# A projection's high weight half against both halves of its input at once

## Chip, cores and metric

The kernel runs on one core of a Trainium2 chip. The metric is the device time of one execution in microseconds; the figure for a kernel is the median of its runs.

## What is computed

Two transformer blocks over 256 tokens of width 1024, in float32. The first block ends in a convolutional gated feed-forward; the second begins with a mixer of two attentions (fox and NSA) whose outputs are merged by sigmoid gates. The change touches the up projection of the one and the merge gates of the other:

```python
def conv_glu_ffn(xn, w_up, conv_w, conv_b, w_down):      # xn = rmsnorm(x), d_ff = 2816
    gu = xn @ w_up
    gate, up = jnp.split(gu, 2, axis=-1)
    gate = causal_dwconv(gate, conv_w) + conv_b.astype(gate.dtype)
    return (jax.nn.silu(gate) * up) @ w_down
...
def hybrid_mixer(h, w_in, ...):                          # h = rmsnorm_2(x)
    proj = h @ w_in
    ...
    g = jax.nn.sigmoid(merge_logit).reshape(B_, S_, N_BRANCH, D_MODEL)
    up = jnp.einsum('bsnc,ncd->bsnd', ys, w_branch)
    merged = jnp.sum(g * up, axis=2)
    return merged @ w_out
```

## The kernel before

Activations lie feature-major: 128 features on the partitions, 8 chunks of them for the width 1024, and the 256 tokens (T) along the free dimension. TensorE multiplies in a reduced format (fp32r), so each float32 operand is split into a high half (the value rounded to fp32r) and a low half (the rest), and each product is three matmuls that add up in one PSUM tile: high weight by high input, high weight by low input, low weight by high input (`mm3`, L346 to 351).

Weights stream in 128x1024 pieces, 4 buffers of each kind: a DMA on SP's queue brings a raw piece `w` (`wraw`), ScalarE copies it to its high half `wh`, and VectorE subtracts to get the low half `wl` (`whalf`, L328). Where the stretch is not marked `calm`, every third subtract goes to GpSimd.

One call of `fm_pair` (L375) makes two chunks of 128 output features for all 256 tokens: 2 chunks x 8 input chunks x 3 matmuls of 128x256, into one 128x512 PSUM tile. The input is the pair of halves of the normed activations, two tiles `xnh` and `xnl` of [128, 8, 256]. The gain is in the halves already; the reciprocal root mean square `r` of each token is multiplied in afterwards, by `fm_norm` (L406), with one VectorE multiply in PSUM (L411), so the projections can start before `r` is known.

There are 8 PSUM banks, 4 buffers called `acc` and 4 called `att`, each 128x512.

In `ffn` (L728) the 4 `acc` buffers hold the output of the down projection over the whole stage. The 22 ups work in `att` buffers: up k makes one chunk of gates and one of ups, so that two ups feed one down. After the multiply by `r`, VectorE does the width-3 convolution of the gate chunk into `fg` (one tensor_scalar, L741, and two multiply-adds, L743), ScalarE the Silu, VectorE the product with the other chunk into `fa` (L746), and after each second up the split of `fa` into `anh` and `anl`. Ups 0 and 1 are done by other helpers since they begin while the norm is still being made; ups 2 to 21 call `fm_norm`. `ffn_order` places a down after each even up from 2 on (down 0 after up 2's issue), the last three at the end. Only the ups up to 3 and from 19 on are `calm`.

In `block2` eight calls of `merge(j)` make the gates, each by `fm_norm` into an `acc` buffer and a ScalarE Tanh into `mg`. They are issued among the steps of the NSA attention: scores on TensorE, maxima on VectorE (L1734), exponentials on ScalarE, reciprocals and scalings on VectorE (L1738, L1743), transposes and the product with the values on TensorE. Between merges 0 and 2 also stands a small softmax over compressed blocks (`L`, L976 to 988), transposed on TensorE (L995) and copied to `PC`.

The order on each engine is set by the Tile scheduler, which places the instructions by its own timeline model; on each engine they then run in that order. A PSUM or SBUF tile's buffer is taken again when all readers of its last holder are done.

Of the kernel before, what the change touches and what calls it, by code (L numbers as in the profile page):

```python
# [21 lines left out]
T = 256  # L22
# [277 lines left out]
class Prog:  # L300
# [89 lines left out]
    def fm_quad(self, x, order, late):  # L390
# [7 lines left out]
                         k == order[0] and c == 0, k == order[-1], skip_group_check=True)  # L398
        return ps

    def first_pair(self, n, **k):

        ps, n.first = n.first or self.fm_pair(n.halves, **k), None
        return ps
# [84 lines left out]

    def pre_norm(self, x, gain):  # L490

        n = Normed(x, *[self.npool.tile([128, 8, T], F32R, tag="xn" + t, name="xn" + t) for t in "hl"])
        self.gain_halves(n, gain)
        return n

# [35 lines left out]
    def post_norm(self, gain):  # L531

        nc, x = self.nc, self.x
        if self.part:
            hs = [self.whalf() for _ in range(2)]
            first = [self.att((128, 512)) for _ in range(2)][::-1]
            self.fm_pair(self.old.halves, ps=first[0], hs=hs)
            self.fm_pair(self.part[1:], ps=first[1], hs=hs)
        n = Normed(x, *[self.npool.tile([128, 8, T], F32R, tag="xn" + t, name="xn" + t) for t in "hl"])
        r = self.rstd(self.pms, self.ptable)  # L540
        self.table = self.ptable
        bc = r[:, None, :].to_broadcast([128, 2, T])
        with self.tc.manual_schedule(engines={mybir.EngineType.DVE}):
            for p in range(5):
                if p < 4:
                    xp, hp = x[:, 2 * p:2 * p + 2], self.hg[:, 2 * p:2 * p + 2]
                    nc.vector.tensor_mul(hp, hp, bc)
                    nc.vector.tensor_add(xp, xp, hp)
                    for k in (2 * p, 2 * p + 1):
                        self.act(n.halves[0][:, k], x[:, k], AF.Identity, scale=gain[:, k:k + 1])  # L550
                for k in (2 * p - 2, 2 * p - 1) if p else ():
                    nc.vector.scalar_tensor_tensor(n.halves[1][:, k], x[:, k], gain[:, k:k + 1],
                                                   n.halves[0][:, k].bitcast(F32), op0=ALU.mult, op1=ALU.subtract)
            if self.part:
                f = [t.rearrange("p (a b) -> p a b", a=2) for t in first]
                t = self.npool.tile([128, 2, T], F32, tag="sq", name="t", bufs=3)
                nc.vector.tensor_mul(t, f[1], bc)
                nc.vector.tensor_add(f[0], f[0], t)
                n.first, self.part = first[0], None
        return n  # L560
# [31 lines left out]
    def build(self):  # L592
        tc, nc = self.tc, self.nc
        with ExitStack() as es:
            pool = lambda name, bufs=1, **k: es.enter_context(tc.tile_pool(name=name, bufs=bufs, **k))
            self.cpool = pool("consts")
            self.pacc = pool("pacc", 4, space=PSUM)
            self.patt = pool("patt", 4, space=PSUM)
            self.dpool = pool("dpool", space=DRAM)
            self.epsc = self.cpool.tile([128, 1], F32, name="epsc")  # L600
            nc.vector.memset(self.epsc, EPS)
            with ExitStack() as big:
                xpool = big.enter_context(tc.tile_pool(name="xpool", bufs=1))
                self.wpool = big.enter_context(tc.tile_pool(name="wpool", bufs=1))
                self.npool = big.enter_context(tc.tile_pool(name="npool", bufs=1))
                self.vec = xpool.tile([128, self.a["vec"].shape[1]], F32, name="vec")
                x = self.x = xpool.tile([128, 8, T], F32, name="x")
                self.table = nc.scalar.preload_act_table_set("natural_log_exp_and_others")
                self.ones = xpool.tile([128, T], F32, name="ones")
                nc.vector.memset(self.ones, 1.0)  # L610
                self.onesd = xpool.tile([128, 128], F32, name="onesd")
                nc.vector.memset(self.onesd, 1.0 / D)

                idle = self.att((128, T))
                for _ in range(8):
                    nc.tensor.matmul(idle, self.onesd, self.ones, start=True, stop=True)

                nc.sync.dma_start(self.vec, self.a["vec"])
                n = Normed(x, *[self.npool.tile([128, 8, T], F32R, tag="xn" + t, name="xn" + t) for t in "hl"])
                gain = self.v("norm_mix_pre")  # L620
                w = self.wpool.tile([128, 1024], F32, tag="w", name="w", bufs=4)
                hi, lo = [self.wpool.tile([128, 1024], F32R, tag=t, name=t, bufs=4) for t in ("wh", "wl")]
                for j in range(2):
                    nc.sync.dma_start(x[:, 4 * j:4 * j + 4], self.a["xT"][:, j * 1024:(j + 1) * 1024])
                    if j == 0:
                        nc.sync.dma_start(w, self.a["W"][0][:, :1024])
                for j in range(2):
                    part = slice(j * 512, j * 512 + 512)
                    nc.vector.tensor_copy(hi[:, part], w[:, part])
                    nc.vector.tensor_sub(lo[:, part], w[:, part], hi[:, part].bitcast(F32))  # L630
                    for k in range(4 * j, 4 * j + 4):
                        self.split(n.halves[0][:, k], n.halves[1][:, k], x[:, k], gain[:, k:k + 1])
                self.wi = 1
                self.ahead = [(hi, lo), self.whalf()]
                self.bd64 = xpool.tile([128, 128], F32, name="bd64")
                nc.gpsimd.memset(self.bd64, 0.0)
                for i in (0, 64):
                    nc.gpsimd.memset(self.bd64[i:i + 64, i:i + 64], 1.0 / 64)
                first = [self.fm_pair(n.halves) for _ in range(2)]
                self.norm_sums(n)  # L640
                self.calm = False
                self.sw = self.cload(xpool, "sw")
                self.c = self.cload(xpool, "cst")
                self.io = self.cload(self.cpool, "cst3")
                self.ident = self.cpool.tile([128, 128], F32, name="ident")
                nc.gpsimd.tensor_copy(self.ident, self.c("ident"))
                n = self.block1_mixer(n, first)
                n = self.cross(n)
                n = self.ffn(n)
                self.block2(n)  # L650
                self.hfp = pool("hfp", side="right")
                self.uvx = es
                self.peer_q()
            self.peer()
# [72 lines left out]

    def ffn(self, n):  # L728
        tc, nc, act = self.tc, self.nc, self.act
        with tc.tile_pool(name="ffn", bufs=1) as fp:  # L730
            hps = [self.acc() for _ in range(4)]
            an, early = {}, []

            def up(k):
                if k % 2 == 0:
                    an[k // 2] = fp.tile([128, 2, T], F32, tag="fa", name="fa", bufs=3)
                if k < 2 and not early:
                    early.extend([self.first_pair(n), self.fm_pair(n.halves, ps=self.att((128, 512)), outer=True)])
                ps = self.fm_norm(n, ready=early[k]) if k < 2 else self.fm_norm(n, ps=self.att((128, 512)))
                g = fp.tile([128, T], F32, tag="fg", name="fg", bufs=3)  # L740
                nc.vector.tensor_scalar(g, ps[:, :T], self.v("fconv2", k), self.v("ffn_conv_b", k), op0=ALU.mult, op1=ALU.add)  # L741
                for d in (1, 2):
                    nc.vector.scalar_tensor_tensor(g[:, d:], ps[:, :T - d], self.v(f"fconv{2 - d}", k), g[:, d:],  # L743
                                                   op0=ALU.mult, op1=ALU.add)
                act(g, g, AF.Silu)
                nc.vector.tensor_mul(an[k // 2][:, k % 2], g, ps[:, T:])  # L746
                if k % 2:
                    an[k // 2] = self.halves(fp, an[k // 2], "an", 3)
# [21 lines left out]
    def block2(self, n):  # L770
# [4 lines left out]
        with tc.tile_pool(name="b2", bufs=1) as bp:  # L775
# [8 lines left out]
            with tc.tile_pool(name="b2a", bufs=1) as ap:  # L784
# [166 lines left out]


                def merge(j):
                    ps = self.fm_norm(n)
                    act(fl(mg[:, 2 * j:2 * j + 2]), ps, AF.Tanh, scale=0.5)


                vb2 = vb.rearrange("p a d -> p (a d)")
# [420 lines left out]
    def block1_mixer(self, n, first):  # L1379
# [4 lines left out]
        with tc.tile_pool(name="mix", bufs=1) as mp:  # L1384
# [293 lines left out]
            for _ in range(2):  # L1678
                step(memory)

            hi, lo = [self.npool.tile([128, 8, T], F32R, tag="xn" + t, name="y" + t) for t in "hl"]
            for j in (3, 1, 2, 0):
                self.split(hi[:, 2 * j:2 * j + 2], lo[:, 2 * j:2 * j + 2], y[:, 2 * j:2 * j + 2])
            order = (6, 7, 2, 3, 4, 5, 0, 1)
# [124 lines left out]
```

## Time and profile before

| | |
|---|---|
| median of 3 runs | 1478.99 us |
| the runs | 1477.73, 1478.99, 1482.02 us |
| the profiled execution's own time | 1478.34 us |
| its span in the profile | 1476.6 us |
| mean granted clock of TensorE | 0.994 |
| TensorE busy | 1437.5 us, 97% of the span |
| VectorE busy | 1079.0 us, 73% |
| ScalarE busy | 782.2 us, 53% |
| GpSimd busy | 223.3 us, 15% |
| instructions | 26774 |

The busy time of an engine is the union of its instructions' spans. Matmuls are pipelined: the recorded length of one (0.28 us for 256 columns) is longer than the interval to the next, so the cost of a matmul in a stream is read from start to start. In the rows below PE is TensorE, DVE VectorE, ACT ScalarE, POOL GpSimd; L411 is line 411; `128x256` is partitions by elements; a bracket at the end gives the idle time before an instruction and what ended it.

### The profile page before, as it was taken

Reading aid. Unit: us, or ns where it says so; the run is one execution under the profiler, and the core shown is the slowest. Engines: PE = TensorE matmul, PEld = TensorE weight load, DVE = VectorE, ACT = ScalarE, POOL = GpSimd, SP = SyncE. Lnnn points to the kernel's source line nnn. Section 1 sums busy time; section 2 is a strip of 40 time slices with the busy share of each in tenths; the row PEclk is TensorE's granted clock in tenths of the full one; section 3 lists DMA queues with packets and bytes.
Section 4 is the critical chain, followed back from the end, with each engine's and each line's share of the span. In section 5 each row is a group of like instructions: output and inputs, shape, how many; then the busy total and the mean of one; then the engine's idle time right before and its main releaser. Section 6 shows DMA issues by size and latency. Waiting matters only on the chain.

```text
span 1476.6 us, 26774 instructions
## 1 busy us (share of the span) xinstructions
PE 1437.5 (97%) x10614; PEld 1336.2 (90%) x10614; DVE 1079.0 (73%) x1996; ACT 782.2 (53%) x1315; POOL 223.3 (15%) x139
## 2 busy tenths in 40 slices
PE   8899898999999999999899999999999999999997
PEld 7798888999999899999899999999998888888886
DVE  7768688766777656669988889778887555655555
ACT  7446466444556756556444545544445445454554
POOL 3731000232200431106341220000000000000000
PEclk9999999999999999999999999999999999999999
DMA  7443432555655433355355545545546555555553
GB/s 255 147 154 116 135 122 86 173 184 179 193 169 192 157 99 131 119 196 177 123 183 163 167 152 185 167 160 170 163 166 221 192 194 191 199 190 195 190 197 128
DMA packets 68245, 246.64 MB, mean 167 GB/s; under 512 B 7540, under 2 KB 8568, under 8 KB 67864
## 3 DMA queue, kind: packets, MB, share of 16 engines
q1 hardware_dynamic: 67544, 243.10, 49.6%
q8 instruction: 83, 1.36, 0.4%
q10 hardware_dynamic: 576, 1.84, 0.3%
q14 instruction: 42, 0.34, 0.1%
HBM read 242.80 MB, written 2.10 MB: 166 GB/s over the span
## 4 chain that ended last, share of the span: by engine, by line
PE 75%; DVE 9%; ACT 1%; issue 1%; POOL 0%; ACTq 0%; DVEq 0%
PE acc L349 20%; PE acc L350 20%; PE acc L351 20%; PE att L350 3%; PE att L351 3%; PE att L349 3%; PE att L1255 2%; DVE wl L328 1%; DVE uvl L1109 1%; PE att L1724 1%; PE acc L1762 1%; DVE ti L1033 1%; DVE tmp L1031 1%; PE att L1751 1%; ACT wh L370 0%
## 5 line engine op out<-in xcount | busy, mean ns | idle before, releaser
L1109 DVE TENSOR_TENSOR uvl<-uv,uvh 128x1024 fp32r<-128x1024 f32 x234 | 291.2, 1244 | 153.5 <-ACT uvh L370 153.3
L370 ACT ACTIVATE uvh<-uv 128x1024 fp32r<-128x1024 f32 x256 | 270.1, 1056 | 235.6 <-PE acc L350 131.1
L370 ACT ACTIVATE wh<-w 128x1024 fp32r<-128x1024 f32 x187 | 196.0, 1057 | 191.5 <-PE acc L350 89.0
L351 PE MATMUL acc<-hh,uvl 128*128 128x256 f32 x1024 | 289.8, 283 | 5.3 <-DVE uvl L1109 4.3
L349 PE MATMUL acc<-hh,uvh 128*128 128x256 f32 x1024 | 294.0, 287 | 0.0
L350 PE MATMUL acc<-hl,uvh 128*128 128x256 f32 x1024 | 289.9, 283 | 0.0
L328 DVE TENSOR_TENSOR wl<-w,wh 128x1024 fp32r<-128x1024 f32 x146 | 184.1, 1267 | 80.1 <-ACT wh L370 79.0
L351 PEld LDWEIGHTS acc<-hh,uvl 128*128 128x128 f32 x1024 | 196.0, 191 | 6.1 <-DVE uvl L1109 4.9
L350 PE MATMUL acc<-uvl,ch 128*128 128x512 f32 x512 | 199.2, 389 | 0.0
L351 PE MATMUL acc<-uvh,cl 128*128 128x512 f32 x512 | 199.2, 389 | 0.0
L350 PEld LDWEIGHTS acc<-hl,uvh 128*128 128x128 f32 x1024 | 196.1, 192 | 0.0
L349 PEld LDWEIGHTS acc<-hh,uvh 128*128 128x128 f32 x1024 | 196.0, 191 | 0.0
L349 PE MATMUL acc<-xnh,wh 128*128 128x256 f32 x544 | 157.3, 290 | 4.7 <-ACT wh L370 3.2
L351 PE MATMUL acc<-xnh,wl 128*128 128x256 f32 x544 | 155.0, 285 | 1.9 <-POOL wl L328 1.2
L350 PE MATMUL acc<-xnl,wh 128*128 128x256 f32 x544 | 155.1, 285 | 0.2
L328 POOL TENSOR_TENSOR wl<-w,wh 128x1024 fp32r<-128x1024 f32 x41 | 100.4, 2448 | 354.3 <-ACT wh L370 352.3
L349 PE MATMUL acc<-uvh,ch 128*128 128x512 f32 x512 | 138.5, 389 | 0.0
L350 PEld LDWEIGHTS acc<-uvl,ch 128*128 128x128 f32 x512 | 96.1, 188 | 19.9
L349 PEld LDWEIGHTS acc<-uvh,ch 128*128 128x128 f32 x512 | 96.1, 188 | 19.9
L351 PEld LDWEIGHTS acc<-uvh,cl 128*128 128x128 f32 x512 | 96.1, 188 | 20.0
L349 PEld LDWEIGHTS acc<-xnh,wh 128*128 128x128 f32 x544 | 104.3, 192 | 8.3 <-ACT wh L370 3.8
L351 PEld LDWEIGHTS acc<-xnh,wl 128*128 128x128 f32 x544 | 104.6, 192 | 3.5 <-POOL wl L328 1.4
(434 smaller groups left out, 2956.4 us busy)
## 6 DMA issues: line engine op xcount, KB each, us to landing
w<-in_W_dram SPq DMA_DIRECT2D x188, 512.0 KB, 4.3
uv<-in_U_dram SPq DMA_DIRECT2D x128, 512.0 KB, 3.6
uv<-in_V_dram SPq DMA_DIRECT2D x128, 512.0 KB, 3.5
mg<-in_cw_dram SPq DMA_DIRECT2D x4, 512.0 KB, 6.9
x<-in_xT_dram SPq DMA_DIRECT2D x2, 512.0 KB, 3.6
mem<-in_memT_dram SPq DMA_DIRECT2D x1, 1024.0 KB, 6.8
sk<-in_W_dram SPq DMA_DIRECT2D x1, 1024.0 KB, 7.5
xd<-xt SPq DMA_DIRECT2D x2, 512.0 KB, 3.1
```

What stands on the lines that cost most here:

```text
L328: (self.nc.gpsimd if pool else self.nc.vector).tensor_tensor(out=lo, in0=w, in1=hi.bitcast(F32), op=ALU.subtract)
L349: mm(ps, wsl(w[0]), xsl(x[0]), start=first, stop=False, **k)
L350: mm(ps, wsl(w[0]), xsl(x[1]), start=False, stop=False, **k)
L351: self.last_mm = mm(ps, wsl(w[1]), xsl(x[0]), start=False, stop=last, **k)
L370: return self.nc.scalar.activation(out, in_, f, **k)
L1031: nc.vector.match_replace(tmp[:, :n], vals[:, 0:8], src, -3.0e38)
L1033: nc.vector.max_index(idx[:, 0:8], vals[:, 0:8], src)
L1109: i = (nc.gpsimd if lo_pool else nc.vector).tensor_tensor(out=lo, in0=w, in1=hi.bitcast(F32), op=ALU.subtract)
L1255: mm(ps[:, j], m1[:, j], m2[:, s * NT + j], start=s == 0, stop=s == 1)
L1724: m = mm(S[i][:, part[blk]], q[rows[i], ch, blk * 128:(blk + 1) * 128], k[rows[i], br if nsa else ch, :128 * (blk + 1)], start=blk == 1, s ...
L1751: nc.tensor.transpose(pt[:, j * 128:(j + 1) * 128], P[:, i, j * 128:(j + 1) * 128], self.ident)
L1762: m = mm(po[rows[i], ch % 2, 128 * blk:], v[:, blk, vc:vc + 64], PT[i][:, 256 * blk:256 + 128 * blk], start=not nsa and blk == 0, stop=blk ...
```

## The change

A new helper `normed` allocates the two halves of the normed input in one tile, [128, 8, 2, 256], so that high and low half of a chunk lie side by side and can be read as 512 consecutive columns. Everything that used the two tiles now uses two strided views of the one.

A new helper `fm_side` takes the place of `fm_norm` in ups 2 to 21 and in the merges. For each of its two chunks it takes a PSUM buffer of its own. For each of the 8 input chunks it issues two matmuls: high weight by both halves, 128x512, whose first 256 columns are the product with the high half and whose last 256 that with the low half; and low weight by the high half, 128x256, added onto the first 256 columns. On the way out ScalarE copies the last 256 columns to SBUF, VectorE adds the first 256 from PSUM, and after both chunks VectorE multiplies by `r` in SBUF. In the ups the result lies in a new SBUF tile `fs` (3 buffers) that the convolution reads; in the merges in `mg` itself, on which Tanh then works in place.

```diff
+    def normed(self, name):
+        t = self.npool.tile([128, 8, 2, T], F32R, tag="xn", name=name)
+        return t[:, :, 0], t[:, :, 1]
+
+    def fm_side(self, n, get, out):
+        mm, (xh, xl) = self.nc.tensor.matmul, n.halves
+        both = [bass.AP(tensor=xh.tensor, offset=xh[:, k].offset, ap=[xh.ap[0], [1, 2 * T]]) for k in range(8)]
+        hs = [self.whalf() for _ in range(2)]
+        for c, (wh, wl) in enumerate(hs):
+            ps = get()
+            for k in range(8):
+                sl = slice(k * 128, k * 128 + 128)
+                mm(ps, wh[:, sl], both[k], start=k == 0, stop=False, skip_group_check=True)
+                self.last_mm = mm(ps[:, :T], wl[:, sl], xh[:, k], start=False, stop=k == 7, skip_group_check=True)
+            self.act(out[:, c], ps[:, T:], AF.Copy)
+            self.nc.vector.tensor_add(out[:, c], out[:, c], ps[:, :T])
+        self.norm_sums(n)
+        self.nc.vector.tensor_mul(out, out, n.r[:, None, :].to_broadcast([128, 2, T]))
...
-        n = Normed(x, *[self.npool.tile([128, 8, T], F32R, tag="xn" + t, name="xn" + t) for t in "hl"])
+        n = Normed(x, *self.normed("xn"))
...
     def ffn(self, n):
...
-                ps = self.fm_norm(n, ready=early[k]) if k < 2 else self.fm_norm(n, ps=self.att((128, 512)))
+                if k < 2:
+                    ps = self.fm_norm(n, ready=early[k])
+                else:
+                    ps = fp.tile([128, 2, T], F32, tag="fs", name="fs", bufs=3)
+                    self.fm_side(n, lambda: self.att((128, 512)), ps)
+                    ps = fl(ps)
...
                 def merge(j):
-                    ps = self.fm_norm(n)
-                    act(fl(mg[:, 2 * j:2 * j + 2]), ps, AF.Tanh, scale=0.5)
+                    o = mg[:, 2 * j:2 * j + 2]
+                    self.fm_side(n, self.acc, o)
+                    act(fl(o), fl(o), AF.Tanh, scale=0.5)
```

In the changed kernel `fm_side` is L406 to 421 and the lines behind it are 22 to 29 higher: the feed-forward's multiply-adds are L771, the product into `fa` L774, the attention's maxima L1763, the reciprocal L1767.

How the instructions stand now is shown at three places. The first is TensorE at the start of up 2, right behind the two matmuls that sum the squares for `r` (`sq`). Before:

```order
L351 MATMUL att<-xnh,wl 128x256
L477 MATMUL att<-sq,onesd 128x256 x2
L349 MATMUL att<-xnh,wh 128x256
L350 MATMUL att<-xnl,wh 128x256
L351 MATMUL att<-xnh,wl 128x256
L349 MATMUL att<-xnh,wh 128x256
```

and of the change:

```order
L351 MATMUL att<-xn,wl 128x256
L499 MATMUL att<-sq,onesd 128x256 x2
L416 MATMUL att<-xn,wh 128x512
L417 MATMUL att<-xn,wl 128x256
L416 MATMUL att<-xn,wh 128x512
```

Two matmuls stand for three, and the order of TensorE's work around them is otherwise the same but for the places where other work is let in between.

The second is VectorE at the start of the ups, from the end of the computation of `r`. Before:

```order
L452 SCALAR_TENSOR_TENSOR rstd<-nt,rstd 128x256
L411 TENSOR_TENSOR att<-att,rstd 128x512 x2
L741 TENSOR_SCALAR fg<-att,vec 128x256 x2
L328 TENSOR_TENSOR wl<-w,wh 128x1024
L743 SCALAR_TENSOR_TENSOR fg<-att,vec,fg 128x255 x2
L411 TENSOR_TENSOR att<-att,rstd 128x512
L743 SCALAR_TENSOR_TENSOR fg<-att,vec,fg 128x254 x2
```

and of the change:

```order
L474 SCALAR_TENSOR_TENSOR rstd<-nt,rstd 128x256
L433 TENSOR_TENSOR att<-att,rstd 128x512 x2
L769 TENSOR_SCALAR fg<-att,vec 128x256 x2
L328 TENSOR_TENSOR wl<-w,wh 128x1024
L771 SCALAR_TENSOR_TENSOR fg<-att,vec,fg 128x255
L419 TENSOR_TENSOR fs<-fs,att 128x256
L771 SCALAR_TENSOR_TENSOR fg<-att,vec,fg 128x255
L771 SCALAR_TENSOR_TENSOR fg<-att,vec,fg 128x254
L328 TENSOR_TENSOR wl<-w,wh 128x1024
L419 TENSOR_TENSOR fs<-fs,att 128x256
```

The two adds of up 2 (L419, into `fs`) stand among the convolution's operations of ups 0 and 1, the first of them behind a low half and one multiply-add.

The third is VectorE at merges 1 and 2, from the sum of the small softmax (`st`, `L`) to the reciprocal of an attention step (`attR`). Before:

```order
L983 TENSOR_REDUCE st<-L 128x16
L984 TENSOR_TENSOR L<-L,cst_5047 128x256
L985 RECIPROCAL st<-st 128x16
L986 TENSOR_TENSOR st<-st,gt 128x16
L411 TENSOR_TENSOR acc<-acc,rstd 128x512
L988 TENSOR_TENSOR L<-L,st 128x256
L328 TENSOR_TENSOR wl<-w,wh 128x1024
L1734 TENSOR_REDUCE attR<-att 128x1 x4
L1738 RECIPROCAL attR<-attR 128x4
```

and of the change:

```order
L1014 RECIPROCAL st<-st 128x16
L328 TENSOR_TENSOR wl<-w,wh 128x1024
L419 TENSOR_TENSOR mg<-mg,acc 128x256
L1015 TENSOR_TENSOR st<-st,gt 128x16
L1763 TENSOR_REDUCE attR<-att 128x1 x2
L421 TENSOR_TENSOR mg<-mg,rstd 128x512
L1017 TENSOR_TENSOR L<-L,st 128x256
L1763 TENSOR_REDUCE attR<-att 128x1 x2
L328 TENSOR_TENSOR wl<-w,wh 128x1024
L419 TENSOR_TENSOR mg<-mg,acc 128x256
L1767 RECIPROCAL attR<-attR 128x4
```

A low half (L328) and the add of a chunk of merge 2 (L419) now stand between the maxima and the reciprocal of the attention step.

The queues of SP and GpSimd hold the same instructions in the same order as before.

## Rows read from the trace of the kernel before

**Rows 1.** Page, section 1: busy us (share of the span) xinstructions.

```profile
PE 1437.5 (97%) x10614; PEld 1336.2 (90%) x10614; DVE 1079.0 (73%) x1996; ACT 782.2 (53%) x1315; POOL 223.3 (15%) x139
```

**Rows 2.** Windows, 272 to 437, 531 to 612: length; busy by engine; clock; DMA.

```profile
272.00:437.00 165.00, 164.89 (x1382) 164.77 (x1381) 114.68 (x162) 78.32 (x100) 34.10 (x14) 1.00 0.58 185
531.00:612.00 81.00, 81.00 (x702) 74.58 (x702) 50.22 (x120) 50.09 (x117) 16.16 (x11) 1.00 0.37 120
```

**Rows 3.** Waits of PE, 250 to 452: total us, times, longest.

```profile
PE att L477 <- DVE sq L464: 2.5, 1, 2.5
PE att L350 <- DVE xnl L552: 2.4, 2, 2.0
```

**Rows 4.** Timeline of PE, a projection of block 2: start us, us, instruction.

```profile
488.01 0.28 PE L349 MATMUL acc<-xnh,wh 128*128 128x256 f32 x1
...
492.57 0.28 PE L351 MATMUL acc<-xnh,wl 128*128 128x256 f32 x1
```

**Rows 5.** Timeline of PE, a 512-wide projection.

```profile
474.04 0.39 PE L351 MATMUL acc<-wh,xnl 128*128 128x512 f32 x1
...
477.67 0.39 PE L349 MATMUL acc<-wh,xnh 128*128 128x512 f32 x1
```

**Rows 6.** Timeline of PE, both widths side by side.

```profile
486.95 0.39 PE L351 MATMUL acc<-wh,xnl 128*128 128x512 f32 x1
487.18 0.28 PE L351 MATMUL acc<-xnh,wl 128*128 128x256 f32 x1
487.29 0.28 PE L349 MATMUL acc<-xnh,wh 128*128 128x256 f32 x1
```

**Rows 7.** Timeline of ACT, at merge 2.

```profile
557.90 1.06 ACT L370 ACTIVATE wh<-w 128x1024 fp32r<-128x1024 f32 x1 [1.07 <-issue]
558.86 0.37 ACT L370 ACTIVATE PC<-att 128x256 f32<-128x256 f32 x1
```

**Rows 8.** DVE groups by form, 272 to 437: busy us, mean ns; idle.

```profile
L411 DVE TENSOR_TENSOR att<-att,rstd 128x512 f32<-128x512 f32 x19 | 13.2, 697 | 7.8 <-PE att L351 7.7
...
L746 DVE TENSOR_TENSOR fa<-fg,att 128x256 f32<-128x256 f32 x20 | 8.4, 418 | 5.1 <-ACT fg L370 5.1
```

**Rows 9.** Timeline of DVE, the last ups.

```profile
409.10 0.70 DVE L411 TENSOR_TENSOR att<-att,rstd 128x512 f32<-128x512 f32 x1 [0.30 <-PE att L351]
...
413.01 1.22 DVE L328 TENSOR_TENSOR wl<-w,wh 128x1024 fp32r<-128x1024 f32 x1 [0.58 <-ACT wh L370]
...
414.86 0.70 DVE L411 TENSOR_TENSOR att<-att,rstd 128x512 f32<-128x512 f32 x1 [0.30 <-PE att L351]
```

**Rows 10.** Timeline of DVE, start of the ups.

```profile
263.88 1.21 DVE L328 TENSOR_TENSOR wl<-w,wh 128x1024 fp32r<-128x1024 f32 x1
265.01 0.86 DVE L743 SCALAR_TENSOR_TENSOR fg<-att,vec,fg 128x255 f32<-128x255 f32 x2
```

**Rows 11.** Timeline of PE, first matmul of up 2; down 0.

```profile
258.98 0.47 PE L349 MATMUL att<-xnh,wh 128*128 128x256 f32 x1
...
272.15 0.39 PE L350 MATMUL acc<-anl,wh 128*128 128x256 f32 x1
```

**Rows 12.** Timeline of DVE, at merge 1.

```profile
556.33 1.01 DVE L1743 TENSOR_SCALAR attP<-attP,attR 128x128 f32<-128x128 f32 x4
```

**Rows 13.** Timeline of PE, at merge 2.

```profile
559.17 0.50 PE L1751 MATMUL att<-ident,attP 128*128 128x128 f32 x3
```

**Rows 14.** Timeline of PE, a projection matmul behind transposes.

```profile
507.39 0.36 PE L349 MATMUL acc<-xnh,wh 128*128 128x256 f32 x1
507.59 0.28 PE L350 MATMUL acc<-xnl,wh 128*128 128x256 f32 x1
```

**Rows 15.** Timelines of DVE and POOL, 319 to 334.

```profile
320.23 0.68 DVE L341 TENSOR_TENSOR anl<-fa,anh 128x512 fp32r<-128x512 f32 x1
...
330.45 2.47 DVE L341 TENSOR_TENSOR anl<-fa,anh 128x512 fp32r<-128x512 f32 x1 [1.83 <-ACT anh L370]
...
329.98 2.40 POOL L328 TENSOR_TENSOR wl<-w,wh 128x1024 fp32r<-128x1024 f32 x1 [6.12 <-ACT wh L370]
```

More of the change, by code (lines that the diff above doesn't have):

```diff
@@ L538, in post_norm @@
             self.fm_pair(self.part[1:], ps=first[1], hs=hs)
-        n = Normed(x, *[self.npool.tile([128, 8, T], F32R, tag="xn" + t, name="xn" + t) for t in "hl"])
+        n = Normed(x, *self.normed("xn"))
         r = self.rstd(self.pms, self.ptable)
@@ L618, in build @@
                 nc.sync.dma_start(self.vec, self.a["vec"])
-                n = Normed(x, *[self.npool.tile([128, 8, T], F32R, tag="xn" + t, name="xn" + t) for t in "hl"])
+                n = Normed(x, *self.normed("xn"))
                 gain = self.v("norm_mix_pre")
@@ L729, in ffn @@
         tc, nc, act = self.tc, self.nc, self.act
+        fl = lambda t: t.rearrange("p a b -> p (a b)")
         with tc.tile_pool(name="ffn", bufs=1) as fp:
@@ L1679, in block1_mixer @@
                 step(memory)
-            hi, lo = [self.npool.tile([128, 8, T], F32R, tag="xn" + t, name="y" + t) for t in "hl"]
+            hi, lo = self.normed("y")
             for j in (3, 1, 2, 0):
```

## Prediction

> **What bounds the kernel now.** I began with the busy shares of the page: TensorE is busy for 1437.5 us of the 1476.6 us span and no other engine comes near [rows 1]. A share is an average, so the next view is that of windows, cut at the two stretches that the change touches [rows 2]. In the ups and downs of the feed-forward (272 to 437 us) TensorE is busy 164.89 of 165.00 us, in the stretch of the merge gates (531 to 612 us) 81.00 of 81.00, both at a granted clock of 1.00. The reader is to see that VectorE (114.68 of 165) and ScalarE (78.32) have room there, and that no transfer is waited for. The view of waits agrees: TensorE's two long waits between 250 and 452 us end before the third up [rows 3]. So here a nanosecond taken from TensorE's own stream is a nanosecond of the end, until something new makes TensorE wait.
>
> **What a k-step costs now and after.** Before, a step is three 128x256 matmuls. In an unbroken run of such matmuls, of another projection of the same input, the first starts at 488.01 and the 39th at 492.57 us: 4.56 us over 38 intervals, 0.120 us each [rows 4]; a step is 0.360 us. After, it is one 128x512 and one 128x256 matmul. The trace has unbroken 128x512 matmuls from a third projection: 17 of them from 474.04 to 477.67 us, 3.63 over 16 intervals, 0.2269 us [rows 5]. The two forms also stand side by side: after a 512-wide start the next, 256-wide one starts 0.23 us later, and the one behind that 0.11 us later [rows 6], so changing width has no price of its own. The new step is 0.2269 + 0.120 = 0.347 us, and saves 0.240 - 0.2269 = 0.0131 us. The columns streamed are the same (768 a step); what goes is one fixed share of a matmul, some 13 ns, and one weight load, which ran beside the matmuls anyway.
>
> There are 20 ups (k = 2 to 21) and 8 merges, each of 2 chunks by 8 steps: 448 steps, of which 320 in the ups and 128 in the merges. 448 x 0.0131 = **5.9 us saved**: 4.2 in the ups, 1.7 in the merges.
>
> The Trainium skill (TensorE: Matmul & The Clock Gate, section Back-to-back issue gap) speaks against this: its formula for the isolated gap is the columns over 2.4 GHz and a constant 2.5 ns, an estimate of 109 ns for 256 columns and 216 for 512. By it a step would save 2.5 ns and the change 1.1 us. The rows have 120 and 227, and the sum goes by the rows.
>
> **What is added.** Each of the 56 chunks gets a ScalarE copy of 128x256 out of PSUM and a VectorE add of the other 256 columns. A like copy took 0.37 us [rows 7], a like VectorE operation with one operand in SBUF and one in PSUM 418 ns; the wide multiply, which now works in SBUF, took 697 ns [rows 8]. So 0.37 us of ScalarE and about 0.42 us of VectorE a chunk (0.70 at most), 0.84 us of VectorE an up. Nothing is taken off for operations that now read SBUF in place of PSUM. Both engines have idle time: VectorE needs 114.68 of 165 us now, and 19 ups add 0.84 x 19 = 16. Priced at zero where TensorE does not wait, and what hides it is TensorE's own stream of matmuls. Its cover is thinnest in the last ups, where VectorE makes all low halves: one up there has a period of 5.76 us with 0.58 + 0.30 idle [rows 9], so it would be 5.76 - 0.88 + 0.84 = 5.72 us, against TensorE's 16 x 0.347 = 5.55. That is 0.17 short an up, for the last three ups; three chunks of slack (3 x 2.78 = 8.3 us) and the last downs take it. SP's and GpSimd's queues keep their order, so no transfer and no GpSimd subtract moves; the other users of the shared halves keep their operations, with a strided operand, priced at zero with the same cover.
>
> **Where TensorE will newly wait.** Every chunk now takes a PSUM buffer to itself, so four buffers hold two ups and not four.
>
> First, the start of the ups. Up 3's first chunk takes the buffer of up 2's first chunk, which is free only after that chunk's add. In VectorE's new order the add stands behind a low half and a convolution operation. The low half ran from 263.88 to 265.01 [rows 10]; with 0.43 for the convolution operation (half of 0.86) and 0.42 for the add it ends at 265.9. TensorE starts up 2 at 258.98 [rows 11] and needs the buffer 5.55 us and a ramp of 0.2 later, at 264.7. It waits 1.2 us. Before, TensorE gave away time here too: the low half of the first down's input ends so late that its second product starts at 272.15 [rows 11]. That chain has two adds more now (0.84), of which the idle time of VectorE takes a part; I set half, 0.4. The saving of the 32 steps ahead (0.42) is lost with it: **0.8 us lost**, 0 to 2.5 as bounds (0 if the buffer comes in time, 2.5 if the 1.2 and the whole 0.84 and 0.42 add up).
>
> Second, merges 1 and 2. ScalarE has a high half and a copy ahead of the last softmax exponentials, VectorE a low half and an add ahead of the reciprocal. Its four scalings then end not at 557.34 but 1.22 + 0.42 = 1.64 us later, 558.98 [rows 9, 12], and at most 1.43 us later still if ScalarE's 1.06 and 0.37 come on top, 560.4 [rows 7]. The transposes that need them start at 559.17 [rows 13], and 47 merge steps ahead of them bring that to 558.5. Late by 0.5 to 1.9: I take a value in the middle, **1.1 us lost**, 0 to 2.5 as bounds (other matmuls can cover it). In merges 3 to 7 a gate is further from the softmax it shares VectorE with, and I see no wait.
>
> Third, about four more changes between transposes and merge matmuls. One interval behind such a change is 0.20 instead of 0.12 us [rows 14]: 4 x 0.08 = **0.3 us lost**.
>
> Sum: -5.9 + 0.8 + 1.1 + 0.3 = -3.7 us from the profiled execution's 1478.34: 1474.6. The median of the runs shown, 1478.99, stands 0.65 above that execution, so the forecast is **1475.3 us**.
>
> **Rivals.**
> - *All of the saving, no visible wait.* For it: the waits are worked out from orders on engines with idle time, and the start already waited before. Against it: the two adds stand in front of something TensorE needs. 1478.99 - 5.9 = 1473.1 us.
> - *The new way out binds.* The copy and the add become the last thing before a buffer is free, and TensorE waits at buffers all through the ups. For it: in the last three, 5.72 against 5.55 us is already more than TensorE leaves. Against it: 8.3 us of slack, refilled at each down. With 0.3 us for each of the 14 ups in which GpSimd helps VectorE the sum is -3.7 + 4.2: 1479.5 us, no change.
> - *Slower: GpSimd holds VectorE.* The wide multiply and the gated product now have both operands in SBUF. A VectorE subtract of that kind took 0.68 us at 320.23 and 2.47 us at 330.45, where GpSimd's subtract ran from 329.98 to 332.38 [rows 15]. It waited until GpSimd was done. The Trainium skill (SBUF — State Buffer, section SBUF: two separate sides) has this as an exclusive lock on a shared pair of ports, and the rows agree. If in the 14 GpSimd windows of the ups [rows 2] such an operation is hit each time and TensorE waits about 1 us for it, that is 14 - 3.7: about 1489 us. It decides from the point where VectorE lies more than the 8.3 us of slack behind TensorE. Against it: one wait is at most 2.40 us, after 6.12 without one [rows 15], and VectorE has idle time between.
> - *The fixed share does not go.* The 512-wide rows come from a product with other operands in the two places (the weights stream there), and with the new tile streaming a wide matmul could cost as much as two narrow ones, 0.240 us. Nothing is saved then and the losses of 2.2 stay: 1478.99 + 2.2 = 1481.2 us. Against it: those rows move the same columns of the same type. (By the formula of the Trainium skill's page TensorE: Matmul & The Clock Gate, Back-to-back issue gap, a saving of 1.1 us, it would be about 1480.)
>
> **How the numbers follow.** My forecast (saving less one to three us of waits, 1473.6 to 1477) gets 0.40, the full saving 0.30, the binding way out 0.17, GpSimd 0.07, the fixed share 0.06. The likeliest time is 1475.3. The range runs from 1472.4 (the full saving and 0.7 for the scatter of a median, as large as the 0.65 above) to 1480.2 (the binding way out and the same 0.7). That leaves out GpSimd's case, most of the fixed share's, and a little of the others at either end, under 2 in 10 together. Of this kernel about 0.3%, 4.4 us, can be told from no change: faster means below 1474.55. That is nearly all of the full saving (0.28) and a third of the forecast's case (0.14): 0.42. Slower is GpSimd's case and the worst of the binding one (0.02): 0.09. The rest, 0.49, is within.
>
> **What the profile after would show.** Right: wide and narrow starts alternate in the ups, a step is 0.347 us, and the stretch that was 165 us is about 4 us shorter; TensorE has a wait of about 1.2 us on a VectorE add near 264.7, another on the scalings near 558.5, and no other above 0.5 us. A step of 0.355 us or more would show the fixed share wrong; waits at buffers up after up the way out; VectorE multiplies of 2 us or more with TensorE waiting behind them GpSimd's case. A gain of over 7 us would mean that I missed a wait that goes away, a loss that I missed one that comes.

## The result and the profile after

The changed kernel takes 1493.06 us (median of 5 runs, 1489.39 to 1500.93) against 1480.35 for the kernel before in the same comparison: 1.0092 of it, 95% interval 1.0071 to 1.0112. It is **slower**, outside the range that was forecast. Its profiled execution took 1493.06 us, its span is 1491.2 us, 14.6 more than before.

Section 1 of its page, beside [rows 1]:

```profile
PE 1443.9 (97%) x10166; PEld 1317.8 (88%) x10166; DVE 1121.7 (75%) x2052; ACT 795.3 (53%) x1371; POOL 225.0 (15%) x139
```

VectorE is busy 42.7 us longer, where 56 adds at 0.42 make 23.5. The views of windows of both kernels, cut at the same five events (first matmul of up 2, first matmul of the downs behind the last up, last step of those downs, last matmul of the projection ahead of the merges, first matmul behind the last merge), show where the span went. Columns: start:end, length, busy us (instructions) of PE, PEld, DVE, ACT and POOL, granted clock, DMA share, GB/s. Before:

```profile
258.98:420.42 161.44, 161.17 (x1346) 160.72 (x1345) 115.62 (x166) 76.30 (x97) 37.91 (x16) 1.00 0.56 183
420.42:437.90 17.48, 17.48 (x148) 17.37 (x147) 11.49 (x18) 10.60 (x15) 0.00 (x0) 1.00 0.57 182
437.90:531.90 94.00, 93.86 (x770) 86.75 (x769) 66.72 (x125) 62.50 (x103) 24.65 (x20) 1.00 0.44 153
531.90:604.40 72.50, 72.50 (x631) 66.53 (x630) 45.21 (x104) 44.94 (x104) 16.16 (x11) 1.00 0.37 119
```

After:

```profile
258.74:425.51 166.77, 160.44 (x1026) 143.18 (x1025) 145.80 (x200) 84.92 (x134) 37.57 (x16) 1.00 0.52 177
425.51:447.20 21.69, 19.48 (x147) 18.97 (x146) 14.16 (x25) 11.73 (x18) 0.00 (x0) 0.92 0.45 146
447.20:541.50 94.30, 94.08 (x771) 86.80 (x770) 67.08 (x124) 62.51 (x103) 25.75 (x20) 1.00 0.44 153
541.50:618.60 77.10, 74.97 (x501) 61.64 (x501) 51.95 (x117) 48.05 (x119) 17.04 (x11) 0.98 0.34 111
```

The ups are 5.3 us longer where 3.4 less was forecast (4.2 saved, 0.8 lost at their start), the last downs are 4.2 longer and the merges 4.6 longer. VectorE has 30 us more in the ups alone, where 40 adds make 17. Before, TensorE had two waits there, 2.5 us on `sq` and this one (view of waits, 255 to 470 us: total, times, longest):

```profile
PE att L351 <- DVE wl L328: 0.2, 1, 0.2
```

Now it has these (the wait on `sq` is the same):

```profile
PE acc L349 <- ACT anh L370: 2.8, 4, 1.6
PE att L417 <- DVE wl L328: 2.7, 3, 1.0
PE att L499 <- DVE sq L486: 2.5, 1, 2.5
PE acc L350 <- DVE anl L341: 2.2, 2, 1.6
PE att L416 <- DVE fs L419: 0.9, 1, 0.9
```

Only the last is a wait on a buffer. The others, but for `sq`, are waits on low halves and splits, for which TensorE hardly waited before. Why these come late stands in VectorE's timeline, here of one stretch (start us, us, instruction, idle before):

```profile
287.82 0.69 DVE L421 TENSOR_TENSOR fs<-fs,rstd 128x512 f32<-128x512 f32 x1
288.55 2.57 DVE L769 TENSOR_SCALAR fg<-fs,vec 128x256 f32<-128x256 f32 x1
291.16 1.00 DVE L771 SCALAR_TENSOR_TENSOR fg<-fs,vec,fg 128x255 f32<-128x255 f32 x2
...
297.62 2.27 DVE L421 TENSOR_TENSOR fs<-fs,rstd 128x512 f32<-128x512 f32 x1
299.92 0.41 DVE L769 TENSOR_SCALAR fg<-fs,vec 128x256 f32<-128x256 f32 x1
300.36 1.00 DVE L771 SCALAR_TENSOR_TENSOR fg<-fs,vec,fg 128x255 f32<-128x255 f32 x2
301.28 1.22 DVE L328 TENSOR_TENSOR wl<-w,wh 128x1024 fp32r<-128x1024 f32 x1
```

GpSimd's and TensorE's, around it:

```profile
288.58 2.40 POOL L328 TENSOR_TENSOR wl<-w,wh 128x1024 fp32r<-128x1024 f32 x1 [5.74 <-DVE fs L421]
296.94 2.39 POOL L328 TENSOR_TENSOR wl<-w,wh 128x1024 fp32r<-128x1024 f32 x1 [5.97 <-ACT wh L370]
```

```profile
301.33 0.39 PE L416 MATMUL att<-xn,wh 128*128 128x512 f32 x1
302.56 0.39 PE L417 MATMUL att<-xn,wl 128*128 128x256 f32 x1 [0.84 <-DVE wl L328]
```

The same multiply takes 0.69 us alone and 2.27 beside a GpSimd subtract, the same first convolution operation 0.41 and 2.57; each ends 0.1 to 0.6 us behind the subtract. A low half for TensorE stands behind the multiply in VectorE's queue, and TensorE waits for it. Beside each of the 15 GpSimd subtracts of the up stretch (269.8 to 400.3 us) one operation on `fs` is that long. Before, the convolution read PSUM and ran beside a subtract (which was at 295.65 to 298.05) at full speed:

```profile
295.32 0.54 DVE L741 TENSOR_SCALAR fg<-att,vec 128x256 f32<-128x256 f32 x1
295.90 1.00 DVE L743 SCALAR_TENSOR_TENSOR fg<-att,vec,fg 128x255 f32<-128x255 f32 x2
297.38 0.42 DVE L746 TENSOR_TENSOR fa<-fg,att 128x256 f32<-128x256 f32 x1 [0.48 <-ACT fg L370]
```

Three theories went into the experiments. **Port**: operations of VectorE on SBUF data wait out GpSimd's subtracts. **Load**: VectorE has too much to do with the adds. For the merges, **place**: their loss is one wait between merges 1 and 2, not a cost of every merge.

### The profile page after: what moved, and what is told of

The parts are those of the page before. It is cut to its first block, busy times and chain, and to the rows that moved or that the text cites. A ratio compares the mean times of both kernels' runs of the same rounds, so it can differ in the third digit from the quotient of the medians.

```text
span 1491.2 us, 25999 instructions
## 1 busy us (share of the span) xinstructions
PE 1443.9 (97%) x10166; PEld 1317.8 (88%) x10166; DVE 1121.7 (75%) x2052; ACT 795.3 (53%) x1371; POOL 225.0 (15%) x139
## 4 chain that ended last, share of the span: by engine, by line
PE 70%; DVE 12%; ACT 2%; issue 1%; POOL 0%; ACTq 0%; DVEq 0%
PE acc L349 19%; PE acc L350 18%; PE acc L351 18%; PE att L416 3%; DVE wl L328 2%; PE att L1284 2%; PE acc L416 2%; DVE fg L771 2%; PE att L417 2%; ACT wh L370 1%; DVE uvl L1138 1%; PE acc L417 1%; PE att L350 1%; PE att L349 1%; PE att L351 1%
## 5 line engine op out<-in xcount | busy, mean ns | idle before, releaser
L328 DVE TENSOR_TENSOR wl<-w,wh 128x1024 fp32r<-128x1024 f32 x146 | 184.7, 1273 | 62.4 <-ACT wh L370 62.0
L328 POOL TENSOR_TENSOR wl<-w,wh 128x1024 fp32r<-128x1024 f32 x41 | 100.5, 2452 | 364.3 <-ACT wh L370 300.1
L349 PE MATMUL acc<-xn,wh 128*128 128x256 f32 x416 | 120.6, 291 | 3.6 <-ACT wh L370 3.6
L351 PE MATMUL acc<-xn,wl 128*128 128x256 f32 x416 | 118.7, 286 | 1.9 <-POOL wl L328 1.5
L350 PE MATMUL acc<-xn,wh 128*128 128x256 f32 x416 | 118.7, 286 | 0.2
L416 PE MATMUL att<-xn,wh 128*128 128x512 f32 x320 | 113.2, 397 | 0.9 <-DVE fs L419 0.9
L417 PE MATMUL att<-xn,wl 128*128 128x256 f32 x320 | 89.7, 281 | 2.7 <-DVE wl L328 2.7
```

The lines of the kernel that those rows point to most:

```text
L328: (self.nc.gpsimd if pool else self.nc.vector).tensor_tensor(out=lo, in0=w, in1=hi.bitcast(F32), op=ALU.subtract)
L349: mm(ps, wsl(w[0]), xsl(x[0]), start=first, stop=False, **k)
L350: mm(ps, wsl(w[0]), xsl(x[1]), start=False, stop=False, **k)
L351: self.last_mm = mm(ps, wsl(w[1]), xsl(x[0]), start=False, stop=last, **k)
L416: mm(ps, wh[:, sl], both[k], start=k == 0, stop=False, skip_group_check=True)
L417: self.last_mm = mm(ps[:, :T], wl[:, sl], xh[:, k], start=False, stop=k == 7, skip_group_check=True)
```

## Experiments

**Each part alone.** `ups_only` puts the merges back on the old path, `merges_only` the ups:

```diff
-                    o = mg[:, 2 * j:2 * j + 2]
-                    self.fm_side(n, self.acc, o)
-                    act(fl(o), fl(o), AF.Tanh, scale=0.5)
+                    ps = self.fm_norm(n)
+                    act(fl(mg[:, 2 * j:2 * j + 2]), ps, AF.Tanh, scale=0.5)
```

> The changed kernel with the eight merges on the old path; only ups 2 to 21 use the wide matmul. In the trace of the changed kernel the lag behind the kernel before was 9.6 us when the feed-forward ended and 14.5 us when the merges had ended. If the two parts add up, this kernel is 8 to 11 us slower than before (about 1489 us). If the loss at the merges is only a consequence of the late feed-forward (another phase of the weight stream), or the other way round, this kernel shows about all 14 us or none of it.

Measured: 1490.84 us, 1.0081 of before (1.0052 to 1.0110).

> The changed kernel with all ups on the old path; only the eight merges use the wide matmul. If the parts add up: 3 to 6 us slower than before (about 1484 us), with one wait of TensorE of about 2 us on the attention's scalings between merges 1 and 2 and a stretch of half clock behind it. If my forecast of the merges was right and their loss comes only from the ups: within 2 us of before.

Measured: 1482.5 us, 1.0035 (1.0020 to 1.0050). Both parts lose by themselves; the sum, 1.0116, is a little above the whole change's 1.0092 and inside what the intervals allow. The merges' loss is no consequence of late ups, and its trace has the same wait of 2.1 us, and a granted clock of 0.66 behind it (561 to 566 us).

**No subtract on GpSimd.** In `no_pool` VectorE makes every low half of the feed-forward:

```diff
-                self.calm = j > 7 if kind == "down" else j < 4 or j > 18
+                self.calm = True
```

> The changed kernel with every low weight half of the feed-forward made by VectorE, none by GpSimd. Theory port: the convolution and the multiply by r, now on SBUF data, wait out GpSimd's subtracts (15 operations of 2.3 to 3.2 us in the trace). Without the subtracts no VectorE operation there takes over 1.3 us; VectorE gets about 27 us back and 14 x 1.22 = 17 us of low halves more, and the kernel is 3 to 8 us faster than the changed one. Theory load: VectorE simply has too much to do, and 17 us more of it make the kernel slower than the changed one by 5 us or more.

Measured: 1481.8 us, 1.0031 (1.0018 to 1.0044). That is 9 us faster than the changed kernel by the two ratios to before, and 11 by the medians, which come from two comparisons; either is more than I expected. VectorE has more operations there (2068 in place of 2052) and TensorE waits less: load falls, as far as the ups' middle is concerned. Its groups of the convolution, 272 to 437 us (busy us, mean ns | idle), against 1170, 1030 and 731 ns on average in the changed kernel for L771 (255 wide), L421 and L769:

```profile
L421 DVE TENSOR_TENSOR fs<-fs,rstd 128x512 f32<-128x512 f32 x19 | 13.1, 690 | 0.2
L771 DVE SCALAR_TENSOR_TENSOR fg<-fs,vec,fg 128x255 f32<-128x255 f32 x19 | 9.1, 480 | 0.2
...
L769 DVE TENSOR_SCALAR fg<-fs,vec 128x256 f32<-128x256 f32 x19 | 7.8, 411 | 0.4
```

The control, the same edit in the kernel before:

> The kernel before with every low weight half of the feed-forward made by VectorE: the control to no_pool. There VectorE operations of the feed-forward wait for a GpSimd subtract only three times (the splits of 2.4 to 2.5 us), and TensorE waits for none of them. So level with before within 1.5 us; if it were 3 us or more faster, part of no_pool's gain would have nothing to do with the change.

Measured: 1478.17 us, 0.9998 (0.9983 to 1.0014). The gain belongs to the change; GpSimd's help was worth nothing to the kernel before.

**The convolution in SBUF, nothing else.** `conv_sbuf` keeps the matmuls, buffers and merges of before, on the change's joined input tile. (`merges_late`, below, has that tile with the old ups, and its ups' stage takes 161.44 us, from 257.27 to 418.71, as long as before: the tile costs nothing.)

```diff
-                    self.fm_side(n, lambda: self.att((128, 512)), ps)
+                    raw = self.fm_pair(n.halves, ps=self.att((128, 512)))
+                    self.norm_sums(n)
+                    nc.vector.tensor_mul(ps, raw.rearrange("p (a b) -> p a b", a=2), n.r[:, None, :].to_broadcast([128, 2, T]))
```

> The matmuls, PSUM buffers and merges of the kernel before; only the multiply by r writes ups 2 to 21 into an SBUF tile, which the convolution and the product read there. No copy and no add is added. Theory port: VectorE operations on that tile take 2 to 3 us wherever a GpSimd subtract runs (about 14 windows), though no wide matmul is there; TensorE, with four ups of buffers, waits for some of it: 0 to 5 us slower than before. Theory load: operations keep their 0.35 to 0.70 us and the time is that of before within 1.5 us.

Measured: 1482.05 us, 1.0025 (1.0010 to 1.0040). The data's move from PSUM to SBUF is enough for VectorE to be held, and the total loses a little by it. Beside 12 of the 15 subtracts of this trace's ups an operation on `fs` is long. GpSimd ran a subtract from 287.17 to 289.57 and another from 295.76 to 298.16, and VectorE

```profile
287.43 2.42 DVE L776 TENSOR_TENSOR fa<-fg,fs 128x256 f32<-128x256 f32 x1 [0.97 <-ACT fg L370]
...
295.86 3.10 DVE L773 SCALAR_TENSOR_TENSOR fg<-fs,vec,fg 128x255 f32<-128x255 f32 x2
```

With deeper buffers and no adds VectorE recovers before TensorE needs it, but for a wait of 0.9 us near 272. That wait is not the whole difference: the ups of this trace are 3.4 us longer than before (257.30 to 422.17 us), and from 258 to 262 us, behind the old wait on `sq`, TensorE's granted clock was 0.59 in place of 1.00. Whether that stretch belongs to the change one trace cannot show.

**The sum kept in PSUM.** `psum_ups`: wide matmuls in the ups, merges old, GpSimd helping; the copy goes to SBUF, the add and the multiply work in PSUM, and the convolution reads there:

```diff
+            low = fp.tile([128, T], F32, tag="fs", name="fs", bufs=4)
+            self.act(low, ps[:, T:], AF.Copy)
+            self.nc.vector.tensor_add(ps[:, :T], low, ps[:, :T])
+            self.nc.vector.tensor_mul(ps[:, :T], ps[:, :T], n.r)
```

> Wide matmuls in the ups, merges on the old path, GpSimd helping as before. The copy of the low product goes to SBUF, but the sum is added into PSUM and multiplied by r there, so that the convolution and the product read PSUM as in the kernel before. VectorE has one operation more an up than in the changed kernel, and a PSUM buffer is held until the convolution is done. Theory port: no VectorE operation of the convolution is held by a GpSimd subtract, the four waits of about 1.0 us on low halves are gone, and the kernel is 4 to 10 us faster than ups_only (1490.84): 1481 to 1487 us. Theory load or buffers: more VectorE work and longer held buffers make it 1491 us or slower.

Measured: 1480.59 us, 1.0000 (0.9984 to 1.0016): faster than `ups_only` by 10 us (medians) or 12 (ratios), at one VectorE operation more an up. This and `no_pool` take away opposite ends of the same collision, and both give back about 10 us. The longer hold of buffers shows once, at the start:

```profile
269.90 0.80 PE L432 MATMUL att<-xn,wh 128*128 128x512 f32 x1 [4.73 <-DVE fa L793]
```

**What a wide matmul saves.** `no_pool_narrow` is `no_pool` with the wide matmul split again:

```diff
-                mm(ps, wh[:, sl], both[k], start=k == 0, stop=False, skip_group_check=True)
+                mm(ps[:, :T], wh[:, sl], xh[:, k], start=k == 0, stop=False, skip_group_check=True)
+                mm(ps[:, T:], wh[:, sl], xl[:, k], start=False, stop=k == 7, skip_group_check=True)
```

> As no_pool (all low halves on VectorE), but the 128x512 matmul is split again into two of 128x256 on the same two halves of the PSUM buffer: copies, adds, buffers and orders stay, only the width goes. If a wide matmul saves a fixed share of 13 ns, this is 448 x 0.0131 = 5.9 us slower than no_pool (1481.8), 1487.7 us; if the step's time is set by its 768 columns alone, the same as no_pool within 1.5 us. The traces of the changed kernel gave a step of 0.347 to 0.360 us, so I expect 2 to 5 us.

Measured: 1481.63 us, 1.0013 (0.9999 to 1.0028), the same as `no_pool`. By the total, width seems worth nothing; the traces say otherwise. Unbroken up matmuls of `no_pool` and of `no_pool_narrow`, first and last:

```profile
356.63 0.39 PE L416 MATMUL att<-xn,wh 128*128 128x512 f32 x1
...
370.50 0.39 PE L416 MATMUL att<-xn,wh 128*128 128x512 f32 x1
```

```profile
363.47 0.28 PE L416 MATMUL att<-xn,wh 128*128 128x256 f32 x1
...
378.35 0.28 PE L417 MATMUL att<-xn,wh 128*128 128x256 f32 x1
```

13.87 us for 40 steps of two is 0.347 us a step; 14.88 us for 124 matmuls is 0.120 each, 0.360 a step. The length of the whole stage from up 2 to the last downs says the same, in `no_pool`, in `no_pool_narrow` and in `ups_inner` (below):

```profile
257.14:415.16 158.02, 157.14 (x1026) 142.81 (x1025) 132.94 (x216) 85.87 (x134) 0.00 (x0) 1.00 0.55 186
261.67:424.06 162.39, 162.26 (x1346) 161.97 (x1345) 134.09 (x216) 85.14 (x134) 0.00 (x0) 0.99 0.55 182
259.72:417.68 157.96, 157.79 (x1090) 146.37 (x1089) 132.00 (x212) 83.76 (x127) 0.00 (x0) 1.00 0.55 186
```

Against 161.44 before, `no_pool` is 3.4 us shorter, just what was forecast for this stage, and 8.8 shorter than the changed kernel. The narrow kernel is 4.4 longer than `no_pool`, with 1.3 us lost to a lower clock at its start against a wait of 1 us in `no_pool`. `ups_inner` saves 3.5 us on its 256 steps, 13.6 ns each. What the narrow kernel loses in the ups it gets back at the merges, where the scheduler chose another order and its trace has no wait on the attention's scalings: from the last step of the downs to the last merge matmul it takes 163.7 us, `no_pool` 167.9. (The narrow kernel's trace is of its longest execution, 1486.47 us.) The total alone was inconclusive.

**Where the merges lose.** `merges_late` has wide matmuls in merges 3 to 7 alone:

```diff
                     o = mg[:, 2 * j:2 * j + 2]
+                    if j < 3:
+                        act(fl(o), self.fm_norm(n), AF.Tanh, scale=0.5)
+                        return
                     self.fm_side(n, self.acc, o)
```

> Wide matmuls in merges 3 to 7 alone. merges_only lost 3.9 us, and its trace shows one wait of 2.1 us on the scalings between merges 1 and 2 and half clock behind it. If that place is the whole loss, this kernel has 80 steps that save 0.0135 us each, 1.1 us, and no wait: within 0 to 1.5 us faster than before. If the copies and adds cost something in every merge, it is 2 us slower.

Measured: 1476.32 us, 0.9989 (0.9973 to 1.0004); its trace has no wait there. Place holds in so far as the loss of `merges_only` (3.9 us by the medians) sits in merges 0 to 2; that it is one wait does not. In the changed kernel's TensorE timeline

```profile
568.26 0.92 PE L1753 MATMUL att<-kr,knq 64*128 64x256 f32 x4
569.11 0.23 PE L870 MATMUL att<-maskb,identb 128*128 128x128 bf16 x1
569.27 0.92 PE L1753 MATMUL att<-kr,knq 64*128 64x256 f32 x4
570.12 0.34 PE L870 MATMUL att<-maskb,identb 128*128 128x128 bf16 x3
572.59 0.30 PE L1780 MATMUL att<-ident,attP 128*128 128x128 f32 x1 [2.13 <-DVE attP L1772]
```

and before

```profile
558.08 0.92 PE L1724 MATMUL att<-kr,knq 64*128 64x256 f32 x8
558.94 0.40 PE L842 MATMUL att<-maskb,identb 128*128 128x128 bf16 x4
```

there are two losses: the wait of 2.13 us, and the attention's score matmuls of two heads, which took 0.86 us for all eight when they stood together and take 0.85 for each four when a mask matmul stands between (twice: at 552.69 and here, some 1 us each). `merges_only` and `no_pool` have the wait and one such split, `merges_late` has neither. That the order causes the split is read from the traces; no run changed it alone.

**Versions without the losses.** `ups_inner` has wide matmuls in ups 4 to 19 alone and no GpSimd subtract, `inner_late` adds merges 3 to 7, and `psum_late` is `psum_ups` with ups 2 and 3 old and merges 3 to 7 wide.

```diff
-                if k < 2:
-                    ps = self.fm_norm(n, ready=early[k])
+                if k < 4 or k > 19:
+                    ps = self.fm_norm(n, ready=early[k]) if k < 2 else self.fm_norm(n, ps=self.att((128, 512)))
```

> Wide matmuls in ups 4 to 19 alone; ups 2, 3, 20 and 21 and all merges on the old path, and no low half of the feed-forward on GpSimd. It takes away the port's blockades, the wait at the start (1.04 us at 264.5 in the changed kernel), the wait on the last split (2.6 us at 436.7) with the half clock behind it, and the merges' wait. What is left is 256 wide steps: at 0.0065 to 0.0131 us each 1.7 to 3.4 us, so 1475.2 to 1477 us, just below before. If VectorE's load still binds, it is at or above before.

> Wide matmuls in ups 4 to 19 and merges 3 to 7, the rest on the old path, no low half of the feed-forward on GpSimd: ups_inner (0.9968 of before) and merges_late (0.9989) together. If the two parts add up: 0.9957, about 1472.5 us. If they hinder each other, 1475 us or more.

> Wide matmuls in ups 4 to 21 with the sum kept in PSUM (as psum_ups) and in merges 3 to 7; GpSimd helps as before. psum_ups was level with before and its trace has one wait of 4.7 us, at 264.9 us, where up 3 needs the buffer of an early up. With ups 2 and 3 on the old path that wait should go, up to 5 us: 0.9955 to 0.998 of before, 1472 to 1476 us. If the buffer is waited for at up 4 in its place, level with before.

Measured: 1475.39 us, 0.9968 (0.9951 to 0.9984); 1474.17 us, 0.9969 (0.9954 to 0.9984); 1473.55 us, 0.9966 (0.9952 to 0.9979). All three beat both kernels, the kernel before by 4.5 to 5 us in the last two. The traces of all three lack the waits of the changed kernel at the start of the ups and on the last split, and the one at the merges. Adding merges 3 to 7 to `ups_inner` could not be told from nothing. In `psum_late` a GpSimd subtract ran from 298.34 to 300.75 beside these:

```profile
298.56 0.43 DVE L436 TENSOR_TENSOR att<-fs,att 128x256 f32<-128x256 f32 x1
298.90 0.47 DVE L790 SCALAR_TENSOR_TENSOR fg<-att,vec,fg 128x254 f32<-128x254 f32 x1
299.29 0.42 DVE L439 TENSOR_TENSOR att<-att,rstd 128x256 f32<-128x256 f32 x1
299.86 0.42 DVE L793 TENSOR_TENSOR fa<-fg,att 128x256 f32<-128x256 f32 x1
```

## Why the prediction was wrong, point by point

- **The saving of a step** was right where nothing disturbs it: worked out as 0.347 us a step from [rows 4, 5, 6], measured as 0.347 in `no_pool`, and the ups' stage there is shorter by the 3.4 us forecast. In the changed kernel's unbroken stretches it was between 0.347 and 0.354 (64 intervals from 290.02 to 301.33 us, 11.31 us for 32 steps). What makes that difference stays open.
- **The start of the ups** was right: TensorE's buffer came 1.04 us late after 264.46, forecast 1.2 near 264.7. The chain behind it was not: `anl` kept TensorE from 271.6 to 273.87, since one of its multiply-adds met a GpSimd subtract at 269.81. I had 0.4 for it.
- **The step that failed** is "Priced at zero where TensorE does not wait, and what hides it is TensorE's own stream of matmuls", together with "three chunks of slack (3 x 2.78 = 8.3 us)". It has two faults. The operations that I moved from PSUM to SBUF were costed by their length alone, while [rows 15] already showed what length they have beside GpSimd. And the slack that I counted is that of PSUM buffers, while TensorE came to wait for low halves and splits, which VectorE makes in the same queue behind the held operations. In the ups TensorE was idle for 6.33 us of the changed kernel's 166.77, against 0.27 before; taking GpSimd's subtracts away gave 8.8 us of the stage back.
- **The GpSimd rival** named this mechanism and was given 0.07. Its time, 1489 us, was meant for the whole change (1493.06). It lies nearest to `ups_only` (1490.84), and by luck, since it came of a price that was too low in one place and too high in another: not two operations an up are exposed but all on `fs`, each subtract held one for 2 us or more, and TensorE felt not 1 us of every one but the waits above. The argument against it ("one wait is at most 2.40 us") took single waits for harmless.
- **The last ups.** I had VectorE 0.17 us an up short and let the last downs take it. TensorE waited 1.60 and 0.61 us for the last split, at 436.70 to 439.92. It did so in `no_pool` too, so GpSimd is not the cause, and not in `ups_inner`, where ups 20 and 21 are on the old path. The way out is longer, and in the fixed order of the queues it is longer than its operations: the last up's multiply by `r` started 3.7 us behind the last up's matmuls (429.20), before 0.2 (420.62), and later VectorE was idle for 1.20 us ahead of a low half at 435.21, which waited for ScalarE, with the last product behind it. How much of it is VectorE's load and how much is order stays open. Behind the waits the clock fell.
- **The merges.** The late scalings were forecast at 1.1 and measured 2.13 us. Not forecast were the split scores, some 2 us, and the clock behind the wait. So a forecast of 0.3 us less for the merges (1.7 saved, 1.1 and 0.3 lost) became 4.6 more.

The rule of the Trainium skill (SBUF — State Buffer, section SBUF: two separate sides) covers both forms seen: an operation with two SBUF inputs, and one in a two-port mode. The trace agrees for the first: L421 with two operands in SBUF took 2.27 us. L769 with one took 2.57; in `no_pool` it takes 411 ns on average, against 543 for L741 of the kernel before, which reads PSUM. That fits a faster mode, but no run shows the mode itself.

## What to carry to other kernels

Ask of an operand that moves from PSUM to SBUF who else works on SBUF at that time: here the same VectorE operation took 0.4 us or 2.6, and the 8.8 us that came back without GpSimd's subtracts are twice what the wide matmul saves in the ups. Measure slack at what the engine at the end waits for, in the order of the queue that makes it, not at the buffer that the change touches. And a saving of 13 ns a matmul is real, but it pays only where the way out is on data and places that hold up nothing else.

## What the runs showed of the hardware

After waits of some 2 us at 436.7 and at 570.1 TensorE ran slower for a while: the granted clock was 0.50, the lower level of 1.2 GHz, in the first of these windows of the changed kernel, and 0.69 on average in the second, but 1.00 behind the 1.6 us wait at 271.6:

```profile
441.00:444.00 3.00, 3.00 (x16) 3.00 (x16) 0.48 (x1) 2.14 (x3) 0.00 (x0) 0.50 0.35 134
572.50:578.00 5.50, 5.41 (x27) 4.09 (x27) 4.09 (x15) 2.24 (x9) 0.00 (x0) 0.69 0.25 97
```

Matmuls of 256 columns started every 0.214 us in the first window (13 intervals between these two) in place of 0.120:

```profile
441.16 0.42 PE L350 MATMUL acc<-anl,wh 128*128 128x256 f32 x1
443.94 0.41 PE L350 MATMUL acc<-anl,wh 128*128 128x256 f32 x1
```

That cost about 1.3 us of the 3.00, and 31% of 5.5 us is 1.7 us in the second, an estimate by the mean clock: well over half of the wait again. A wait on TensorE has to be priced with what may follow it. It need not follow: behind the wait of 2.5 us on `sq`, which stands in every kernel here, the clock was 1.00 before and in the changed kernel, but 0.59 (258 to 262 us) in `conv_sbuf` and 0.61 (261.67 to 266 us) in `no_pool_narrow`. What decides it stays open.
